# Side work in a planned transformer layer: new prices and gates for the planner, fewer VectorE operations, the first two output blocks in halves

## The chip, the cores and the metric

One core of one Trainium2 chip. The metric is the device time of one execution in microseconds (us); the time of a kernel is the median of its runs. Engine names are those of the profile: PE is TensorE's matmuls and PEld its weight loads, DVE is VectorE, ACT is ScalarE, POOL is GpSimd, SP is SyncE.

## The reference

One inference step of one decoder layer for a prompt of 256 tokens and 8 sample tokens (264 columns in all), in fp32, with a model width of 2048:

```
x = x + W_out[ RGLRU-group(xn) || mLSTM-group(xn) ],  xn = RMSNorm(x), one projection xn @ w_in
x = x + CrossAttn(RMSNorm(x), memory K/V)             (4 heads, 256 memory tokens)
x = x + SwiGLU(RMSNorm(x))
y = RMSNorm_final(x)
```

What the change touches lies in the first line. The RG-LRU group (8 blocks of 128 channels) takes a causal convolution of width 4 over the tokens, two sigmoid gates r and i from block-diagonal matrices, and a linear recurrence:

```
log_a = -8 * r * softplus(-lam);  a = exp(log_a)
mult  = sqrt(max(1 - exp(2 * log_a), 0));  bx = mult * (i * xr)
h_t   = a_t * h_(t-1) + bx_t                 # over the 256 prompt tokens, one step for a sample token
y_rg  = rmsnorm(h * gelu(z_gate), g_rg_out)
```

The mLSTM group (4 heads, keys of 128, values of 256) has an input gate and a log-sigmoid forget gate per token and head, a stabilised chunkwise form for the prompt, and for each sample token one update of a 128 x 256 state:

```
C = sc * C + k v^T;  n = sc * n + k;  h = (q C) / max(|q n|, exp(-m))
y_ml = rmsnorm(h, g_ml_out) * sigmoid(z_o)
```

## The kernel before

All matmuls of the big projections are made in three passes of fp32r: a weight is split into a high part (ScalarE, a copy) and a low part (VectorE, raw minus high), the activations likewise, and `mm3` adds high x high, high x low and low x high. Activations lie transposed, with channels on partitions and the 264 tokens on columns.

The work is a list `steps` of weight blocks. A step is one output block of 128 channels: 16 chunks of 128 x 128, so 48 matmuls of 264 columns. Steps 0 to 3 take the first four recurrence blocks by chunks of the input, steps 4 to 7 the other four, step 8 the mLSTM gates (32 matmuls), 9 to 16 queries and keys, 17 to 24 values, 25 to 32 the RG output gates (`evac_rgg`), 33 to 40 the mLSTM output gates, 41 to 56 the output projection W_out, 57 to 72 the queries of the cross attention. Then follow memory keys and values, the attention's output, and the SwiGLU.

SP loads the blocks ahead (`load_piece`, a ring of five raw half blocks), and `split_half` splits the block of the next step into two of four `w` tiles, at high priority. A finished PSUM bank (four of tag `mm`, four of tag `ax`) is read by the step's evacuation, which is held in `pend` and emitted at the next step.

Everything else is **side work**: Python generators that emit a few instructions at a time between two steps. `rg_gen` makes the recurrence, `ml_gates` the gate sums, `ml_prompt`, `ml_values` and `ml_heads` the prompt's heads, `ml_sample` the 32 sample blocks (8 tokens x 4 heads), `ml_norm` the mLSTM group's norm, `rg_out` the RG group's, `mem_gen` the memory's norm. A generator yields a number after a piece, and `STEP` where it wants to wait for the next step. `Engine` adds a price in us for each instruction to a clock per engine (`price_dve`, `price_act`, `price_pe`); before each step the clocks of DVE and ACT are raised to that of PE, and `pump` lets the generators go on, in the order of their priorities, while both clocks are below PE's clock plus 0.5. Where a step names a `need`, `finish` empties that generator first.

This is the order of emission. The framework's scheduler then orders the instructions on ACT, DVE, PE and POOL by priority along a timeline that it simulates, and sets the semaphores; only SP's order is written by hand. On the chip each engine works its list off in order, so an instruction that waits holds what stands behind it.

Small tiles come from rings: `tmp` from six tiles of tag `t`, `ctile` from eight tiles of 16 columns, and `dw` and `ds` (two each) serve the cross attention of the sample tokens, which starts in the steps after 57.

Places that the change touches: the planner (`price_dve` line 63, `price_act` line 71, `Gen.run` line 275, `pump` line 291); `log1p`; `evac_rgx` and `rg_conv` (lines 491 and 510), which scale a recurrence block out of PSUM and convolve it; `rg_gen` (526); `rg_out` (588), which uses `rstd_wide`: one fp32 matmul with a matrix of ones, and Newton steps over 264 columns, where `rstd_from` sums per token into three columns, does its steps there and spreads the result by matmuls; `evac_if` and `ml_gates`, with rows of 4 heads x 264 tokens; the mask in `ml_prompt`; the temporaries of `ml_sample`; `proj` (930), where the spread of the first norm's factor is put between two chunks of steps 5 and 6; `evac_first`; the steps of W_out; and the main loop (1378).

Of the kernel before, what the change touches and what calls it, by code (L numbers as in the profile page):

```python
# [10 lines left out]
F32 = mybir.dt.float32  # L11
# [6 lines left out]
P = 128  # L18
# [45 lines left out]
def price_dve(name, n, a, k):  # L64
    fast = name in ("tensor_scalar", "tensor_copy", "tensor_single_scalar", "memset")
    if name == "tensor_reduce":
        n = int(np.prod(a[1].shape[1:]))
    return 0.07 + n * (0.00052 if fast else 0.0066 if name == "reciprocal" else 0.00104)


def price_act(name, n, a, k):
    return 0.12 + n * 0.00083

# [7 lines left out]
def layer_kernel(ctx: ExitStack, tc, xT, memT, vec, wrg, w_in, w_out, w_q, w_k, w_v, w_o,  # L81
# [189 lines left out]
    class Gen:  # L271
        def __init__(self, g, prio=0):
            self.g, self.done, self.prio = g, False, prio

        def run(self, go):
            while not self.done and go():
# [5 lines left out]
                if y is STEP:  # L282
                    break

    def side(g, prio=0):
# [5 lines left out]
    def pump(until):  # L291
        go = lambda: dve.clock < until and act.clock < until
        for x in list(gens):
            if x.prio < 0:
                with tc.high_priority():
                    x.run(lambda: True)
# [173 lines left out]
    def log1p(out, e):  # L470

        w = e.shape[-1]
        pp = e.shape[0]
        s = tmp(w)[:pp]
        q = tmp(w)[:pp]
        dve.tensor_scalar(q, e, 2.0, None, op0=OP.add)
        dve.reciprocal(q, q)
        dve.tensor_mul(s, e, q)
        s2 = tmp(w)[:pp]
# [11 lines left out]
    def evac_rgx(n):  # L491
        def f(ps):
            if n == 0:
                rg["xr"] = Arr(RGB)
            z = B([P, 2, 292])
            zi = z[:, 0, :]
            dve.memset(zi[:, 0:3], 0.0)
            smp = zi[:, 259:291].rearrange("p (b j) -> p b j", j=4)
            hist = V("cst", n * 24, 24).rearrange("p (b j) -> p b j", j=3)
            act.activation(smp[:, :, 0:3], hist, AF.Copy)  # L500
            p2, m = unturn(ps[:, :N]), N // 2
            dve.tensor_mul(zi[:, 3: 3 + m], p2[:, 0, :], rstd[:, :m])
            dve.tensor_mul(zi[:, 3 + m: 259], p2[:, 1, : T - m], rstd[:, m:T])
            dve.tensor_mul(smp[:, :, 3:4], p2[:, 1, T - m:].rearrange("p (b j) -> p b j", j=1),
                           rstd[:, T:N].rearrange("p (b j) -> p b j", j=1))
            rg["z", n] = z
            rg["zn"] = n + 1
        return f

    def rg_conv(n):  # L510
        z = rg.pop(("z", n))
        zi, t = z[:, 0, :], z[:, 1, :]
        smp = zi[:, 259:291].rearrange("p (b j) -> p b j", j=4)
# [4 lines left out]
        dve.scalar_tensor_tensor(t[:, :288], zi[:, 1:289], w[1], t[:, :288], op0=OP.mult, op1=OP.add)  # L518
        dve.scalar_tensor_tensor(t[:, :288], zi[:, 2:290], w[2], t[:, :288], op0=OP.mult, op1=OP.add)
        xr = rg["xr"](n)  # L520
        dve.scalar_tensor_tensor(xr[:, :T], zi[:, 3:259], w[3], t[:, :T], op0=OP.mult, op1=OP.add)
        ts = t[:, 259:291].rearrange("p (b j) -> p b j", j=4)
        dve.scalar_tensor_tensor(xr[:, T:N].rearrange("p (b j) -> p b j", j=1), smp[:, :, 3:4], w[3],
                                 ts[:, :, 0:1], op0=OP.mult, op1=OP.add)

    def rg_gen():
# [5 lines left out]
        for n in range(RGB):  # L532
            while rg["zn"] <= n:
                yield STEP
            rg_conv(n)
            yield STEP
            for t, j, b in ((r, 0, "ba"), (ig, 1, "bx")):
                ps = bank("ax")
                pe.matmul(ps[:, :N], wr[j][:, n, :], rg["xr"](n), start=True, stop=True)
                last = act.activation(t(n), ps[:, :N], AF.Sigmoid, bias=V(b, n))  # L540
            yield 0.1
# [4 lines left out]
        for n in range(RGB):  # L546
            with tc.issue_after(last.ins):
                act.activation(e2(n), r(n), AF.Exp, scale=c[:, 8 + n: 9 + n])
                le = act.activation(r(n), r(n), AF.Exp, scale=c[:, n: n + 1])
            dve.tensor_scalar(e2(n), e2(n), 1.0, -1.0, op0=OP.min, op1=OP.add)  # L550
            dve.tensor_mul(ig(n), ig(n), xr(n))
            yield 0.8
        for n in range(RGB):
            with tc.issue_after(le.ins):
                act.activation(e2(n), e2(n), AF.Sqrt, scale=-1.0)
            dve.tensor_mul(ig(n), ig(n), e2(n))
# [65 lines left out]
    def evac_if(ps):  # L622
        R = Arr(7)
        ml["R"] = R
        for q in range(2):
            pool_e.memset(R.tile(q), 0.0)
        li, u, a, b = (R(j)[0:4] for j in range(4))
        act.activation(halves(a), unturn(ps[64:68, :N]), AF.Copy)
        act.activation(halves(b), unturn(ps[96:100, :N]), AF.Copy)
        dve.tensor_add(halves(li), unturn(ps[0:4, :N]), halves(a))  # L630
        dve.tensor_add(halves(u), unturn(ps[32:36, :N]), halves(b))
        dve.tensor_mul(li, li, rstd[0:4, :])
        dve.tensor_mul(u, u, rstd[0:4, :])
        dve.tensor_scalar(li, li, V("bi")[0:4], None, op0=OP.add)
        dve.tensor_scalar(u, u, V("bf")[0:4], None, op0=OP.add)
        ml["gates"] = side(ml_gates(), 1)

    mrow = const.tile([4, 1 + NS], F32, name="mrow")
    gcol = const.tile([P, 2, H], F32, name="gcol")
# [3 lines left out]
    def ml_gates():  # L643
        R = ml["R"]
        li, u, e, lf, b, g, M = (R(j)[0:4] for j in range(7))
        yield STEP
        dve.scalar_tensor_tensor(e, u, -1.0, u, op0=OP.mult, op1=OP.min)
        act.activation(e, e, AF.Exp)
        yield 0.4
        log1p(lf, e)  # L650
        yield 6.0
        dve.tensor_scalar(u, u, 0.0, None, op0=OP.min)
        dve.tensor_sub(lf, u, lf)

# [28 lines left out]
        act.activation(gcol, ps[:, 64:72].rearrange("p (j h) -> p j h", h=H), AF.Copy)  # L683
        act.activation(emc, ps[:, 72:84], AF.Exp, scale=-1.0)
        yield 0.1
# [27 lines left out]
    def ml_prompt():  # L713
# [13 lines left out]
        for h in range(H):  # L727
# [13 lines left out]
            act.activation(E, E, AF.Exp)  # L741
            dve.tensor_mul(E[:, 0:128], E[:, 0:128], mask)
            dve.tensor_mul(E[:, 256:384], E[:, 256:384], mask)
            dve.tensor_mul(Pm, sps[:, 0:384], E)
# [57 lines left out]
    def ml_sample():  # L802
# [127 lines left out]
    def proj(src, rhs, evac, cols=2048, n=N, need=()):  # L930

        def f(i):
# [3 lines left out]
            for c in range(nch):  # L936
                if (i, c) in ((5, 9), (6, 3)):
                    with tc.high_priority():
                        st["rstd_x"].run(lambda: True)
                mm3(ps[:, :n], w(c), rhs(c), c == 0, c == nch - 1)  # L940
# [15 lines left out]
    def evac_first(_):  # L956
        for n in range(4):
            evac_rgx(n)(first[n])
# [93 lines left out]

    for m in range(KC):
        proj(w_out[m], ry, residual(m, "g_xa", "xa", norm_wide),
             need=("rgout", "ng") if m == 0 else ())

# [312 lines left out]
    with tc.high_priority(), in_order():  # L1369
# [4 lines left out]
        split_half(0, 1)  # L1374

    pend = []
    kept = ExitStack()
    for i, (src, cols, pef, evf, need) in enumerate(steps):
        if i > 1:
            load_piece(i + LD - 1)  # L1380
        if i == 7:
            st["rg"] = side(rg_gen(), 0)
        if "ng" in need:
            with tc.high_priority(300):
# [156 lines left out]
```

## Time and profile before

| | us |
|---|---|
| median of 3 runs (lowest to highest) | 1469.44 (1466.56 to 1472.32) |
| the profiled execution | 1467.96 |
| its span, first to last instruction | 1466.2 |
| TensorE busy in it | 1442.1 |
| VectorE busy | 1063.2 |
| ScalarE busy | 790.1 |
| GpSimd busy | 129.5 |
| mean granted clock of TensorE | 0.995 |

The profile is of one execution. A row of a timeline or of a group names engine, operation, the tile written and the tiles read (`w<-raw` is a weight split, `mm<-B,w` a big matmul, `t<-mm,rstd` the evacuation of an RG gate), its shape, a count, and the idle time of the engine ahead of it with what ended that idle time. Times in a timeline are us from the span's start. Almost all instructions are recorded by one helper, so all have the line L60, and tiles tell them apart.

### The profile page before, as it was taken

What the parts mean: (1) busy time and instruction counts of PE and PEld (TensorE: products, weight loads), DVE (VectorE), ACT (ScalarE), POOL (GpSimd) and SP (SyncE); (2) the same over time, 40 slices, a digit from 0 to 9 for tenths busy, and PEclk for the clock granted to TensorE, in tenths of its full rate; (3) what the DMA queues carried; (4) which work ended last, traced back from release to release, by engine and by line L of the source; (5) the groups of instructions that cost most, each with busy time, mean ns of one, the idle gap of its engine ahead of it and who ended that gap; (6) DMA issues with size and microseconds to landing.
All of it is one profiled execution on the core that took longest, in us unless ns stands there. A gap on an engine that the chain in (4) does not pass through costs nothing.

```text
span 1466.2 us, 30098 instructions
## 1 busy us (share of the span) xinstructions
PE 1442.1 (98%) x12049; PEld 1417.3 (97%) x12049; DVE 1063.2 (73%) x2046; ACT 790.1 (54%) x1252; POOL 129.5 (9%) x195
## 2 busy tenths in 40 slices
PE   9998999999999999999999999999999999999997
PEld 8998898999999999999999999999999999999997
DVE  7986788998799999986675656555565655556564
ACT  7566685666466666665544444344444434444463
POOL 0000220000124344320000000000000000000000
PEclk9999999999999999999999999999999999999999
DMA  9654896447699978855555555555555555555563
GB/s 290 212 186 158 271 318 237 169 173 245 247 351 344 342 287 336 343 206 185 195 196 189 199 195 195 201 190 199 192 197 199 190 202 189 199 195 194 174 191 114
DMA packets 99757, 326.02 MB, mean 222 GB/s; under 512 B 10944, under 2 KB 19824, under 8 KB 99616
## 3 DMA queue, kind: packets, MB, share of 16 engines
q1 hardware_dynamic: 83616, 269.84, 52.7%
q0 software_dynamic: 15136, 53.16, 10.0%
q8 instruction: 94, 1.54, 0.4%
q10 hardware_dynamic: 864, 1.09, 0.2%
q14 instruction: 47, 0.39, 0.1%
HBM read 312.78 MB, written 11.28 MB: 221 GB/s over the span
## 4 chain that ended last, share of the span: by engine, by line
PE 92%; DVE 3%; ACT 2%; DMA 2%; issue 1%; SPq 0%; DVEq 0%; ACTq 0%
PE mm L60 87%; PE ax L60 4%; DVE B L60 2%; DVE w L60 1%; DMA raw<-w_in 1%; ACT w L60 1%; ACT B L60 1%; DMA o_sc<-B 0%; DMA B<-scr 0%; DVE t L60 0%; ACT L60 0%; ACT t L60 0%; SPq L199 0%; SPq L1354 0%; DVE c L60 0%
## 5 line engine op out<-in xcount | busy, mean ns | idle before, releaser
L60 PE MATMUL mm<-B,w 128*128 128x264 f32 (+1 forms) x10960 | 1285.9, 279 | 7.1 <-DVE t L60 3.6
L60 PEld LDWEIGHTS mm<-B,w 128*128 128x128 f32 x10960 | 1264.6, 190 | 16.2 <-issue 4.6
L60 DVE TENSOR_TENSOR w<-raw,w 128x1024 fp32r<-128x1024 f32 (+1 forms) x522 | 623.1, 1195 | 298.9 <-ACT w L60 298.2
L60 ACT ACTIVATE w<-raw 128x1024 fp32r<-128x1024 f32 (+1 forms) x522 | 536.2, 1029 | 550.9 <-PE mm L60 381.9
L60 PE MATMUL mm<-w,B 128*128 128x512 f32 x384 | 86.5, 380 | 0.0
L60 PEld LDWEIGHTS mm<-w,B 128*128 128x128 f32 x384 | 70.7, 189 | 9.4
L1433 POOL TENSOR_TENSOR B<-B,rstd 128x264 f32<-128x264 f32 x4 | 2.8, 736 | 802.9 <-ACT rstd L60 802.9
L60 DVE TENSOR_TENSOR t<-mm,rstd 128x264 f32<-128x264 f32 x96 | 41.4, 432 | 28.7 <-PE mm L60 28.7
L60 DVE SCALAR_TENSOR_TENSOR B<-B,dw 128x256 f32<-128x256 f32 x128 | 53.0, 466 | 2.8 <-ACT dw L60 2.6
L60 DVE TENSOR_TENSOR xres<-xres,mm 128x264 f32<-128x264 f32 (+1 forms) x81 | 34.2, 423 | 27.0 <-PE mm L60 27.0
L60 DVE SCALAR_TENSOR_TENSOR dw<-B,qsm,dw 128x256 f32<-128x256 f32 x96 | 49.0, 516 | 0.8
L60 PE MATMUL ax<-B,B 128*128 128x256 f32 (+3 forms) x288 | 46.3, 302 | 1.2 <-DVE B L60 1.2
L1104 POOL TENSOR_TENSOR ds<-dw,ds 128x256 fp32r<-128x256 f32 x32 | 37.5, 1172 | 105.2 <-ACT ds L60 105.1
L60 PEld LDWEIGHTS ax<-B,B 128*128 128x128 f32 x288 | 39.9, 191 | 3.3 <-DVE B L60 1.4
L60 ACT ACTIVATE B<-xres,vecs 128x264 fp32r<-128x264 f32 (+1 forms) x64 | 32.2, 503 | 6.3 <-DVE xres L60 4.6
L60 ACT ACTIVATE t<-xres 128x264 f32<-128x264 f32 (+1 forms) x53 | 21.1, 408 | 15.9 <-DVE xres L60 15.9
L1093 POOL DMA_DIRECT2D B<-kcT x32 | 17.4, 543 | 122.0 <-DVE B L60 109.1
L60 DVE SCALAR_TENSOR_TENSOR B<-xres,vecs,B 128x264 fp32r<-128x264 f32 x48 | 23.3, 486 | 4.1 <-ACT B L60 4.1
L60 ACT ACTIVATE t<-B,B 128x128 f32<-128x128 f32 x64 | 21.4, 390 | 7.4 <-DMA B<-scr 7.3
L60 ACT ACTIVATE dw<-B,qsm 128x256 f32<-128x256 f32 x32 | 16.2, 507 | 16.8 <-issue 7.8
L60 ACT ACTIVATE B<-t 128x264 fp32r<-128x264 f32 (+1 forms) x60 | 24.1, 408 | 1.5 <-DVE t L60 1.5
L60 ACT ACT_TABLE_LOAD x18 | 23.1, 1283 | 2.6 <-PEq L1513 1.7
(168 smaller groups left out, 689.2 us busy)
## 6 DMA issues: line engine op xcount, KB each, us to landing
raw<-w_gu SPq DMA_DIRECT2D x176, 512.0 KB, 3.7
raw<-w_d SPq DMA_DIRECT2D x80, 512.0 KB, 3.7
raw<-w_in SPq DMA_DIRECT2D x74, 512.0 KB, 4.6
raw<-w_out SPq DMA_DIRECT2D x32, 512.0 KB, 4.1
B<-kcT POOLq DMA_DIRECT2D x32, 512.0 KB, 8.8
raw<-w_q SPq DMA_DIRECT2D x32, 512.0 KB, 4.4
B<-vcT POOLq DMA_DIRECT2D x32, 512.0 KB, 9.8
raw<-w_k SPq DMA_DIRECT2D x32, 512.0 KB, 5.3
```

The source lines that it names most:

```text
L60: return f(*a, **k)
L1093: pool_e.dma_start(kc, kcT[h, b])
L1104: pool_e.tensor_sub(ws[:, 1], acc, ws[:, 0].bitcast(F32))
L1433: e.tensor_mul(st["y"](c), st["y"](c), r)
```

## The change

It does the following.

- **Planner.** The prices get rates for reciprocal and scan, a larger fixed part for `scalar_tensor_tensor` and for accumulating operations, for a per-partition scale on ScalarE, and 1.28 for a change of ScalarE's function table. They hold up to step 57; after it the old ones come back. A generator is now stopped only by the clock of an engine that its last piece used, and after a `STEP` its first piece always goes.
- **Recurrence.** An evacuation reads the bank in one product instead of three, the first product of the convolution goes to ScalarE, `1 - exp(2 log_a)` becomes a Relu on ScalarE, the memsets go to POOL. Two blocks are convolved in one step, and their four sigmoids follow together.
- **mLSTM gates.** Both gates are scaled in one tile of 36 partitions; the log-sigmoid is made after a turn by matmuls, on 12 columns, and turned back. The exponential of `emc` moves to the first head of `ml_prompt`.
- **Norm of the RG group** by `rstd_from`; **mask** by one operation a head; **sample blocks** take their temporaries from `dw` and `ds`.
- **First norm.** Its factor is spread at chunk 8 of step 6 instead of chunk 3, and the bank of tag `mm` is read first.
- **W_out.** Blocks 0 and 1 first take their RG chunks (0 to 7); only then is the mLSTM norm finished, and the other chunks of both follow.

The diff, cut:

```diff
 def price_dve(name, n, a, k):
...
+    rate = {"reciprocal": 0.0066, "tensor_tensor_scan": 0.00208}.get(name, 0.00052 if fast else 0.00104)
+    fixed = 0.12 if name == "scalar_tensor_tensor" else 0.07
+    return fixed + n * rate + (0.08 if "accum_out" in k else 0.0)
...
 def price_act(name, n, a, k):
-    return 0.12 + n * 0.00083
+    func, load = a[2] if len(a) > 2 else k.get("func"), 0.0
+    if func in (AF.Exp, AF.Sqrt, AF.Sigmoid, AF.Gelu_apprx_tanh, AF.Silu) and func != TABLE["at"]:
+        TABLE["at"], load = func, 1.28
+    by_column = not isinstance(k.get("scale", 1.0), (int, float))
...
+    return load + (0.2 if by_column else 0.12) + n * 0.00083 + (0.2 if "accum_out" in k else 0.0)
...
-        go = lambda: dve.clock < until and act.clock < until
+        go = lambda used: not (used[0] and dve.clock >= until or used[1] and act.clock >= until)
...
     def evac_rgx(n):
...
-            dve.memset(zi[:, 0:3], 0.0)
+            pool_e.memset(zi[:, 0:3], 0.0)
...
-            dve.tensor_mul(zi[:, 3: 3 + m], p2[:, 0, :], rstd[:, :m])
-            dve.tensor_mul(zi[:, 3 + m: 259], p2[:, 1, : T - m], rstd[:, m:T])
-            dve.tensor_mul(smp[:, :, 3:4], ...)
+            dve.tensor_mul(halves(zi[:, 3: 3 + N]), unturn(ps[:, :N]), halves(rstd))
+            act.activation(smp[:, :, 3:4], zi[:, 3 + T: 3 + N].rearrange("p (b j) -> p b j", j=1), AF.Copy)
...
     def rg_conv(n):
...
-        dve.tensor_scalar(t[:, :288], zi[:, 0:288], w[0], V("cb", n), op0=OP.mult, op1=OP.add)
+        act.activation(t[:, :296], zi[:, 0:296], AF.Identity, scale=w[0], bias=V("cb", n))
...
     def rg_gen():
...
             rg_conv(n)
+            yield 1.5
+            if n % 2 == 0:
+                continue
             yield STEP
-            for t, j, b in ((r, 0, "ba"), (ig, 1, "bx")):
+            for q in (n - 1, n):
+                for t, j, b in ((r, 0, "ba"), (ig, 1, "bx")):
...
-            dve.tensor_scalar(e2(n), e2(n), 1.0, -1.0, op0=OP.min, op1=OP.add)
+                act.activation(e2(n), e2(n), AF.Relu, scale=-1.0, bias=ones[:, 0:1])
...
     def rg_out():
-        yield from rstd_wide(acc_rg, rr, RGB * P)
+        yield from rstd_from(acc_rg, rr, RGB * P)
...
     def ml_gates():
+        for j, w0 in enumerate(WIN):
+            pe.matmul(ps[:, 4 * j: 4 * j + 4], R(0)[:, w0: w0 + P], ident[:, 32:36], start=True, stop=True)
...
+        for j, (lo, hi) in enumerate(((0, P), (P, T), (T, N))):
+            pe.matmul(ps[0:4, lo:hi], lu[:, 4 * j: 4 * j + 4], ident[:, P - (hi - lo):], start=True, stop=True)
...
     def ml_sample():
-                    t2 = tmp(256).rearrange("p (v d) -> p v d", d=P)
+                    t2 = sb.tile([P, 264], F32, tag="dw", bufs=2, name=nm("dw"))[:, 0: T]
...
-                    j = tmp(P)
+                    j = sb.tile([P, 2, T], F32R, tag="ds", bufs=2, name=nm("ds"))[:, 0, 0: P].bitcast(F32)
...
-                if (i, c) in ((5, 9), (6, 3)):
+                if (i, c) in ((5, 9), (6, 8)):
...
+    def pe_out(m):
+        def f(i):
+            ps, w = bank(), W(i)
+            kept_out[m] = (ps, w)
+            for c in range(RGB):
+                mm3(ps[:, :N], w(c), ry(c), c == 0, False)
+            if m == 1:
+                finish(lambda: st["ng"].done)
+                for c in range(RGB, KC):
+                    for q in range(2):
+                        mm3(kept_out[q][0][:, :N], kept_out[q][1](c), ry(c), False, c == KC - 1)
+            return ps
...
+        if i == 57:
+            PACE["full"] = False
```

More of the change, by code (lines that the diff above doesn't have):

```diff
@@ L272, in __init__ @@
         def __init__(self, g, prio=0):
-            self.g, self.done, self.prio = g, False, prio
+            self.g, self.done, self.prio, self.used = g, False, prio, (False, False)
         def run(self, go):
-            while not self.done and go():
+            while not self.done and go(self.used):
+                was = dve.clock, act.clock
                 try:
@@ L282, in run @@
                 if y is STEP:
+                    self.used = False, False
                     break
+                self.used = dve.clock > was[0], act.clock > was[1]
     def side(g, prio=0):
@@ L626, in evac_if @@
             pool_e.memset(R.tile(q), 0.0)
[L627 to L636, printed above, removed]
+        x, a = R(0)[0:36], R(1)[0:36]
+        act.activation(gbias[0:4], V("bi")[0:4], AF.Copy)
+        act.activation(gbias[32:36], V("bf")[0:4], AF.Copy)
+        act.activation(halves(a), unturn(ps[64:100, :N]), AF.Copy)
+        dve.tensor_add(halves(x), unturn(ps[0:36, :N]), halves(a))
+        dve.tensor_mul(x, x, rstd[0:36, :])
+        dve.tensor_scalar(x, x, gbias[0:36], None, op0=OP.add)
+        ml["gates"] = side(ml_gates(), 0)
+    gbias = const.tile([P, 1], F32, name="gbias")
+    pool_e.memset(gbias, 0.0)
     mrow = const.tile([4, 1 + NS], F32, name="mrow")
@@ L644, in ml_gates @@
         R = ml["R"]
[L645 removed]
+        li, e, lf, b, g, M = (R(j)[0:4] for j in (0, 2, 3, 4, 5, 6))
         yield STEP
[L647 to L648 removed]
+        ps = bank("ax")
+        for j, w0 in enumerate(WIN):
+            pe.matmul(ps[:, 4 * j: 4 * j + 4], R(0)[:, w0: w0 + P], ident[:, 32:36], start=True, stop=True)
+        u, eu, lu = ctile(12), ctile(12), ctile(12)
+        act.activation(u, ps[:, 0:12], AF.Copy)
+        dve.scalar_tensor_tensor(eu, u, -1.0, u, op0=OP.mult, op1=OP.min)
+        act.activation(eu, eu, AF.Exp)
         yield 0.4
[L650 to L651 removed]
+        log1p(lu, eu)
         dve.tensor_scalar(u, u, 0.0, None, op0=OP.min)
[L653 removed]
+        dve.tensor_sub(lu, u, lu)
+        yield 2.0
+        yield STEP
+        ps = bank("ax")
+        for j, (lo, hi) in enumerate(((0, P), (P, T), (T, N))):
+            pe.matmul(ps[0:4, lo:hi], lu[:, 4 * j: 4 * j + 4], ident[:, P - (hi - lo):], start=True, stop=True)
+        act.activation(lf, ps[0:4, :N], AF.Copy)
         one = ones[0:4, 0:1].to_broadcast([4, T])
@@ L956, in evac_first @@
     def evac_first(_):
-        for n in range(4):
+        for n in (3, 0, 1, 2):
             evac_rgx(n)(first[n])
@@ L1051, in ry, with evac_out, g @@
         return st["yrg"](c) if c < 8 else st["yml"](c - 8)
-    for m in range(KC):
-        proj(w_out[m], ry, residual(m, "g_xa", "xa", norm_wide),
-             need=("rgout", "ng") if m == 0 else ())
+    kept_out = {}
+    def pe_out(m):
[10 more added lines that the diff above has]
+            return ps
+        return f
+    def evac_out(m):
+        f = residual(m, "g_xa", "xa", norm_wide)
+        def g(ps):
+            if m == 1:
+                residual(0, "g_xa", "xa", norm_wide)(kept_out[0][0])
+            if m > 0:
+                f(ps)
+        return g
+    for m in range(2):
+        steps.append((w_out[m], 2048, pe_out(m), evac_out(m), ("rgout", "pend") if m == 0 else ()))
+    for m in range(2, KC):
+        proj(w_out[m], ry, residual(m, "g_xa", "xa", norm_wide))
     qn = {"n": 0}
@@ L1374, in layer_kernel @@
         split_half(0, 1)
+    PACE["full"], TABLE["at"] = True, None
     pend = []
```

55 lines of the change are left out of this document (30 added, 25 removed).

## The prediction

> **What bounds the kernel now.** I read the busy times of the whole span first, then TensorE's waits, then stretches around them, then the instructions there. The windows view, its columns the busy time of each engine with the instructions in brackets, then the granted clock, the DMA share and GB/s:
>
> ```profile
> core 0: us, PE busy (x) PEld busy (x) DVE busy (x) ACT busy (x) POOL busy (x), PEclk, DMA share, GB/s
> 0.00:1466.20 1466.20, 1442.08 (x12049) 1417.25 (x12049) 1063.21 (x2046) 790.05 (x1252) 129.47 (x195) 1.00 0.63 222
> 121.60:135.40 13.80, 9.66 (x58) 8.79 (x58) 11.66 (x25) 9.54 (x18) 0.00 (x0) 0.75 0.25 87
> 231.10:240.40 9.30, 9.25 (x57) 7.59 (x58) 7.63 (x22) 6.37 (x18) 2.66 (x5) 0.84 0.67 232
> ```
>
> TensorE is busy for 1442.1 of 1466.2 us, so no other engine's saved work can count by itself. Only TensorE's waits, and what follows from them, can be won. The view of waits for TensorE (total, times, longest):
>
> ```profile
> PE ax L60 <- DVE B L60: 4.0, 3, 1.7
> PE mm L60 <- DVE t L60: 3.6, 1, 3.6
> PE mm L60 <- ACT w L60: 2.0, 1, 2.0
> PE ax L60 <- ACT w L60: 1.9, 3, 1.1
> PE ax L60 <- DVE c L60: 1.6, 1, 1.6
> PE mm L60 <- DVE w L60: 1.5, 2, 1.1
> ```
>
> TensorE's timeline shows where they lie (start, us, instructions, idle time before with its releaser):
>
> ```profile
> 44.39 0.81 PE L60 MATMUL ax<-ident,c 128*128 128x128 f32 x6 [1.56 <-DVE c L60]
> ...
> 128.75 0.90 PE L60 MATMUL ax<-ident,B 128*128 128x128 f32 x3 [1.07 <-DVE B L60]
> 129.31 0.79 PE L60 MATMUL mm<-B,w 128*128 128x264 f32 x2
> 131.19 15.19 PE L60 MATMUL mm<-B,w 128*128 128x264 f32 x116 [1.10 <-DVE w L60]
> ...
> 205.73 21.85 PE L60 MATMUL mm<-B,w 128*128 128x264 f32 x192
> 231.15 5.47 PE L60 MATMUL mm<-B,w 128*128 128x264 f32 x34 [3.57 <-DVE t L60]
> ...
> 263.78 2.07 PE L60 MATMUL ax<-ident,c 128*128 128x128 f32 x18
> 265.71 38.05 PE L60 MATMUL mm<-B,w 128*128 128x264 f32 x336
> ```
>
> The run of 192 gives the undisturbed price: 21.85 / 192 = 0.1138 us a matmul, 48 x 0.1138 = 5.46 us a step. Four losses stand out, all inside the first projection (steps 0 to 40).
>
> **A**, in step 6: 1.56 us, TensorE waits for the last small VectorE operation of the RMS factor.
>
> **B**, in step 19: the waits of 2.0 (ACT w), 1.07 and 1.10, together 4.2 us. Then the clock: it was granted at 0.75 in that window, and 116 matmuls took 15.19 where 116 x 0.1138 = 13.20 would do, 2.0 us more. B is 6.2.
>
> **C**, in steps 25 and 26: what is left of the first row, 4.0 - 1.07 = 2.9 us.
>
> **D**, ahead of step 33: 3.57 us; then 34 matmuls in 5.47 instead of 3.87 at a clock of 0.84, 1.6 us. D is 5.2.
>
> Sum: 1.6 + 6.2 + 2.9 + 5.2 = 15.9 us. This is about all that the change can reach; from 265.71 on, 336 matmuls run without a wait, over the start of the output projection (three steps later, near 282).
>
> Here the trace and the Trainium skill differ. "TensorE: Matmul & The Clock Gate", section "HAM oscillation", speaks of no idle gaps over about 3.4 us. In B the clock fell although its longest single gap is 2.0, so the sum of gaps seems to count. By the rule B would hold no clock loss, and the forecast below would be 2.0 us smaller.
>
> **Why B happens.** ScalarE's timeline:
>
> ```profile
> 119.58 1.04 ACT L60 ACTIVATE w<-raw 128x1024 fp32r<-128x1024 f32 x1
> 120.53 1.72 ACT L60 ACTIVATE B<-B,rgc 128x264 f32<-128x264 f32 x4
> 122.27 1.28 ACT L60 ACT_TABLE_LOAD   x1
> 123.56 2.30 ACT L60 ACTIVATE B<-B 128x264 f32<-128x264 f32 x7
> 125.77 1.04 ACT L60 ACTIVATE w<-raw 128x1024 fp32r<-128x1024 f32 x1
> ```
>
> Two weight splits (w<-raw) lie 6.2 us apart, more than a whole step, with recurrence work and a table load between them. The planner prices these exponentials at 0.34 us and the load at nothing; measured are 1.72 / 4 = 0.43 and 1.28. It believes that there is room and emits too much into one step.
>
> **Why D happens.** VectorE's timeline, then the operations on tile bcs (count, duration, first and last start):
>
> ```profile
> 230.58 0.43 DVE L60 TENSOR_TENSOR t<-mm,rstd 128x264 f32<-128x264 f32 x1
> ```
>
> ```profile
> L60 DVE SCALAR_TENSOR_TENSOR B<-B,bcs,t x32: 475/479/486, 159.6 to 233.1; 128x256 f32<-128x256 f32 x32
> ```
>
> The first row is the evacuation of step 29, whose matmuls were the first 48 of the 192 and ended near 211.2. It came 19 us later, and without it no PSUM bank was free for step 33 (four banks). It waited for nothing that the row names. I take it to be the ring of six "t" tiles: the gate's z, the mLSTM sample blocks' t2 and their product j all come out of it, and in that stretch each block takes two.
>
> **The change, part by part.**
>
> *Spread from chunk 3 to chunk 8 of step 6.* Fifteen matmuls, 1.7 us, go ahead of the waiting one. The wait of 1.56 is covered: -1.6. The evacuations behind it start no later, since the chain on VectorE ends when it did.
>
> *t2 and j moved to the tiles dw and ds.* Nothing else uses these before the queries' projection. The ring holds only gate work then, and D goes whole: -5.2. The price is two buffers in place of six: ScalarE's t2 of one block waits for VectorE's use of two blocks before. VectorE is the slower of the two, so I take 0; if not, it falls under the second rival.
>
> *Prices, gates, pairs.* VectorE's groups (mean ns):
>
> ```profile
> L60 DVE TENSOR_TENSOR w<-raw,w 128x1024 fp32r<-128x1024 f32 x488 | 599.8, 1231 | 294.8 <-ACT w L60 294.1
> ...
> L60 DVE SCALAR_TENSOR_TENSOR t<-B,B 128x128 f32<-128x128 f32 x64 | 18.4, 288 | 1.5
> ...
> L60 DVE DVE_READ_ACCUMULATOR t<-B,B 128x1 f32 x64 | 5.2, 81 | 0.0
> ...
> L60 DVE TENSOR_SCALAR B<-B,vecs 128x288 f32<-128x288 f32 x8 | 3.1, 422 | 0.0
> ...
> L60 DVE TENSOR_SCALAR B<-B 128x264 f32<-128x264 f32 x8 | 2.4, 298 | 2.1 <-ACT B L60 1.4
> ```
>
> A sample block was priced 0.336 + 2 x 0.203 = 0.742 and is now 0.386 + 2 x 0.333 = 1.052; measured is 0.479 + 2 x (0.288 + 0.081) = 1.22. A step leaves VectorE, by the planner, 5.47 - 2.27 for two splits - 0.35 for an evacuation = 2.85 us. That was 3.8 blocks a step, 4.7 us of real work, beside two splits of 1.23 and an evacuation of 0.43: 7.6 us asked of 5.46. With the new price it is 2.7 blocks, 3.3 us, 6.2 in all: still over, by much less, and the rows are durations, which overlap by some 0.1 us. So C shrinks but I doubt that it goes: I take its longest wait, -1.7, and leave 1.2. In B the exponentials become 0.42 each and the load 1.28, so the burst spreads over three steps; both ScalarE's wait and VectorE's wait for w should go, and with them the clock loss, while the 1.07 behind DVE B is a chain of its own: -5.1.
>
> *Fewer VectorE operations.* The convolution's first product (8 x 0.422 = 3.4 us) and the subtraction (8 x 0.298 = 2.4) move to ScalarE; log1p runs over 12 columns instead of 264. VectorE's saved time counts nothing by itself: TensorE's work hides it, outside B and C. ScalarE takes 16 operations of about 0.43, 6.9 us over a dozen steps, and some small copies. Also hidden if spread; if they land ahead of a split, second rival. Eight 3-column memsets go to POOL, idle in that window: 0.
>
> *More matmuls.* The gates' two turns (6 fp32 matmuls) and the RG group's norm by columns (6) give 24 short TensorE instructions; six such took 0.81 at 44.39, and spaced at 0.1138 24 make 2.7 us. The one wide sum they replace is not set off. +2.7, with 0 (they fall into waits) and 3.2 as ends.
>
> *Two output blocks in halves.* There is no wait at 282 to cover: 0 now. It costs nothing either, unless all four w tiles being held delays step 43; its first half is free after 24 matmuls and has 72 (8.2 us) to be split.
>
> Sum: -1.6 - 5.2 - 1.7 - 5.1 + 2.7 = -10.9 us. The profiled execution took 1467.96, so 1457.1; the median of the runs stands 1.5 above it, which makes **1458.5**. If all four losses go and the matmuls are free, 1469.4 - 15.9 = 1453.5.
>
> **Rivals.** *ScalarE becomes late instead.* The page "ScalarE: Activation LUTs" of the Trainium skill, section "Rules for kernel authors", wants relu, mul and add on VectorE; that speaks against this move. In rows: ahead of a split like that at 125.77 stand eight more operations of 0.43, 3.4 us. Then B and C stay, A and D go: -1.6 - 5.2 + 2.7 = -4.1, 1465.3; with B deeper by 3.4, 1468.7. For it: ScalarE was the releaser of B. Against it: the new prices count these operations. About 1467, no change.
>
> *The sample blocks starve (slower).* Blocks now run from 159.6 to 233.1, 73.5 us; the norm's spreads follow at 263.78, 31 us later, and the output projection needs them by 282 + 5.5 for the half steps = 287.5, less some 8 us for the products after the spreads: 16 us of slack. The dearer price alone stretches 73.5 by 1.052 / 0.742 to 104, 31 us more. Then TensorE waits 15 us in step 42 and loses 2.0 by the clock as in B: -10.9 + 17 = +6.1, 1475.5, and more if dw and ds slow it too. It decides at 16 us of delay. For it: prices only rise. Against it: blocks were held up by the ring and by bursts, not by their price alone, since 32 in 73.5 us are 2.4 a step, below the 2.7 that the new price allows.
>
> **How the numbers follow.** The forecast, with all-gone as its best end: 0.68, faster. ScalarE late: 0.18, same. Starving: 0.10, of which 0.06 over the bound and 0.04 within. Not named: 0.04, slower. Half a per cent, 7.3 us, is about what a measurement can tell here, so faster is 0.68, same 0.22, slower 0.10. The range runs from 1452 (all-gone, with half the 3 us by which the lowest run lies under the median) to 1470, which takes in ScalarE late with 1.3 for the same spread.
>
> **What would show it.** Right: no wait <-DVE t; the eight gate evacuations each within a step of their matmuls; no ACT stretch of 6 us between splits near the Exp; the clock at 1.00 from 60 to 280; the last sample block before 250. Wrong: the wait at 44.39 moved instead of gone; TensorE waiting for ACT w or DVE B for over 4 us in sum; a wait in the second half of step 42.

## The result, and the profile after

| | before | after |
|---|---|---|
| median of 5 runs, us (lowest to highest) | 1469.44 (1466.56 to 1472.32) | 1456.42 (1455.83 to 1456.79) |
| ratio, 95% interval | | 0.9915 (0.9900 to 0.9929) |
| the profiled execution, us | 1467.96 | 1455.83 |
| its span, us | 1466.2 | 1454.1 |
| mean granted clock of TensorE | 0.995 | 0.998 |

The changed kernel is 13.0 us faster by the medians, 12.1 us by the profiled executions. The forecast was 1458.5, in a range of 1452 to 1470. The runs also lie closer together: 1.0 us apart instead of 5.8. One of the eleven runs of a kernel below, that with the ring undone, took 3921.74 us and is left out of its ratio.

The windows view of after, for the whole span and for the window of B:

```profile
0.00:1460.00 1460.00, 1439.19 (x12071) 1415.52 (x12071) 1045.10 (x1999) 794.90 (x1279) 128.31 (x204) 1.00 0.63 223
121.60:135.40 13.80, 11.89 (x100) 11.35 (x99) 13.38 (x27) 8.72 (x18) 3.42 (x7) 1.00 0.66 183
```

In the second row 100 matmul instructions stand where before had 58, and the clock is 1.00 where it was 0.75. Nowhere between the start and 1449.7 us is a clock under 1.00 granted. Before had two stretches at 0.5 there: 6.8 us from 128.2 and 3.4 us from 230.6.

The view of TensorE's waits (total, times, longest):

```profile
PE mm L60 <- DVE w L60: 2.1, 2, 1.9
PE ax L60 <- ACT w L60: 2.1, 3, 1.5
PE mm L60 <- DVE ones L60: 1.1, 1, 1.1
PE ax L60 <- DVE B L60: 0.8, 1, 0.8
```

With two more of 0.3 this sums to 6.7 us; before it was 16.0. The wait for `t` (D) and that for `c` of 1.56 (A) are gone, the waits for `B` fell from 4.0 to 0.8. TensorE's timeline shows the four places:

```profile
44.08 0.73 PE L60 MATMUL ax<-ident,c 128*128 128x128 f32 x6
...
71.50 0.73 PE L60 MATMUL ax<-ident,B 128*128 128x4 f32 x6
...
82.48 0.64 PE L60 MATMUL ax<-ident,c 128*4 128x128 f32 x6
...
124.25 0.38 PE L60 MATMUL ax<-ident,B 128*128 128x128 f32 x2
126.52 3.19 PE L60 MATMUL mm<-B,w 128*128 128x264 f32 x26 [1.89 <-DVE w L60]
...
154.50 1.14 PE L60 MATMUL ax<-B,B 128*128 128x258 f32 x4 [0.81 <-DVE B L60]
...
188.18 43.45 PE L60 MATMUL mm<-B,w 128*128 128x264 f32 x384
231.46 0.72 PE L60 MATMUL ax<-ones,acc_rg 128*128 128x1 f32 x6
...
239.49 0.73 PE L60 MATMUL ax<-ident,c 128*128 128x128 f32 x6
```

The spread at 44.08 has no idle time ahead of it (A). At 126.52 one wait of 1.89 is left of B, at 154.50 one of 0.81 of C. At 188.18 stand eight whole steps without a wait, 43.45 / 384 = 0.113 us a matmul, over the place of D. The rows of six at 71.50, 82.48, 231.46 and 239.49 are the new short matmuls (E).

So the account of the span: waits 16.0 - 6.7 = 9.3 us; 10.2 us at half clock lose half, 5.1, less some 1.1 that were waits themselves (0.5 us of the wait of 1.07, all of that of 1.10 and 0.5 us of that of 3.57 lie inside the stretches, and half of these 2.2 us would count twice); and 1.5 back for matmul time, as the comparison with the kernel of four parts below gives it. 9.3 + 4.0 - 1.5 = 11.8 of the 12.1.

### The profile page after: what moved, and what is told of

Its sections match the earlier page's. It is cut to its first block, busy times and chain, and to the rows that moved or that the text cites. A ratio compares the mean times of both kernels' runs of the same rounds, so it can differ in the third digit from the quotient of the medians.

```text
span 1454.1 us, 30126 instructions
## 1 busy us (share of the span) xinstructions
PE 1439.2 (99%) x12071; PEld 1415.5 (97%) x12071; DVE 1045.1 (72%) x1999; ACT 794.9 (55%) x1279; POOL 128.3 (9%) x204
## 3 DMA queue, kind: packets, MB, share of 16 engines
q0 software_dynamic: 15136, 53.16, 10.2%
## 4 chain that ended last, share of the span: by engine, by line
PE 94%; ACT 2%; DMA 1%; DVE 1%; issue 1%; SPq 0%; POOL 0%; DVEq 0%; POOLq 0%
PE mm L60 90%; PE ax L60 5%; DMA raw<-w_in 1%; ACT B L60 1%; DVE B L60 1%; DMA B<-scr 0%; ACT w L60 0%; DVE w L60 0%; ACT L60 0%; SPq L213 0%; ACT dw L60 0%; DVE ds L60 0%; SPq L1412 0%; DMA scr<-lt 0%; ACT t L60 0%
## 5 line engine op out<-in xcount | busy, mean ns | idle before, releaser
L60 PEld LDWEIGHTS mm<-B,w 128*128 128x128 f32 x10960 | 1260.6, 189 | 10.7 <-DVE w L60 2.4
L60 ACT ACTIVATE dw<-B,B 128x128 f32<-128x128 f32 x64 | 20.9, 390 | 7.1 <-DMA B<-scr 6.3
L60 ACT ACTIVATE dw<-ax,dw 128x256 f32<-128x256 f32 x32 | 15.0, 470 | 17.7 <-DVE dw L60 14.0
```

Source lines behind the costliest of these rows:

```text
L60: return f(*a, **k)
```

## The experiments

The question was which parts make the gain. The theory of the forecast adds losses that are independent of each other: the ring cures D, chunk 8 cures A, the prices cure B and C. Its rivals: the parts need each other; the exponentials merely move; the sample blocks starve. First four parts were done alone on the kernel before, then parts were undone one by one in the kernel after, then a set of four was put on before. The gate alone was not run, nor the pairs or the halves alone. In all, ratios are to the kernel before on the same chip, with 95% intervals; where runs on different chips are set side by side, it is by these ratios. A ratio on record is not the quotient of the two medians; the two differ by up to 0.0012, 1.8 us.

**The ring alone** (on before; the same for `j`, on `ds`):

```diff
-                    t2 = tmp(256).rearrange("p (v d) -> p v d", d=P)
+                    t2 = sb.tile([P, 264], F32, tag="dw", bufs=2, name=nm("dw"))[:, 0: T]
+                    t2 = t2.rearrange("p (v d) -> p v d", d=P)
```

> The kernel before, with only the two temporaries of the sample blocks moved from the six-tile ring t to the tiles dw and ds. My theory (the ring holds back the gate evacuations): the wait of 3.57 us behind DVE t goes, the eight gate evacuations come within a step of their matmuls, no half clock after it; about 5.2 us less, 1464 against 1469. Rival (VectorE is simply over-asked by underpriced blocks): the evacuations stay 9 to 19 us late, 0 us.

Measured: 1465.30 us, ratio 0.9969 (0.9958 to 0.9981), which is 4.6 us. The wait for `t` is gone, and the sample blocks run faster than before, to 218.1 instead of 233.1:

```profile
L60 DVE SCALAR_TENSOR_TENSOR B<-B,bcs,dw x32: 473/478/485, 158.1 to 218.1; 128x256 f32<-128x256 f32 x32
```

So D was the ring, and two buffers do not slow the blocks. C, with 2.56 us in sum hardly smaller than before (2.88), now has one wait of 2.02. TensorE's timeline, then the window just behind that wait:

```profile
179.31 4.09 PE L60 MATMUL ax<-B,B 128*128 128x256 f32 x12 [2.02 <-DVE B L60]
```

```profile
179.40:182.60 3.20, 3.20 (x10) 2.75 (x11) 3.20 (x12) 2.21 (x4) 0.24 (x1) 0.50 0.74 252
```

A half-clock stretch of 3.4 us, which D had before, stands here now, and takes back a part of the gain.

**Chunk 8 alone** (on before):

```diff
-                if (i, c) in ((5, 9), (6, 3)):
+                if (i, c) in ((5, 9), (6, 8)):
```

> The kernel before, with only the spread of the first norm's factor put at chunk 8 of step 6. My theory: the wait of 1.56 us goes and nothing follows it, 1.6 us less. Rival (the first evacuations come later by as much and TensorE waits for a bank in steps 7 to 9): the wait moves, 0 us.

Measured: 1468.84 us, ratio 0.9990 (0.9978 to 1.0002). The wait at 44 is gone from its trace, but the time shows it only as a hint: in the profiled execution, the longest of its runs, the half-clock stretch of B lasts 10.2 us instead of 6.8, one more of 3.4 stands at 176.7, and that of D lasts 6.8. A cured wait of 1.56 is within what these stretches vary by.

**The prices alone** (on before, up to step 57 as in the change: `price_dve`, `price_act` and the switch `PACE`; gate, operations and tiles as before):

> The kernel before, with only the new price functions (up to step 57); the gate of the planner, the operations and the rings stay. My theory (waits B and C come from work emitted too densely because it is underpriced): B loses 5.1 of its 6.2 us and C 1.7 of 2.9, so about 6.8 less; D stays, since the ring stays. Rival (the number of VectorE operations sets B and C): 0 us.

Measured: 1469.23 us, ratio 0.9997 (0.9988 to 1.0007), 0.4 us where 6.8 were expected. Most of B and all of D are gone: the longest wait at B's place is 1.07, and no wait for `t` is left although the ring is the old one. What they brought was paid back. The operations on `bcs`, TensorE's timeline, and the window behind the wait:

```profile
L60 DVE SCALAR_TENSOR_TENSOR B<-B,bcs,t x32: 471/478/485, 158.4 to 274.2; 128x256 f32<-128x256 f32 x32
```

```profile
272.12 2.74 PE L60 MATMUL mm<-B,w 128*128 128x264 f32 x22 [1.22 <-DVE w L60]
...
288.17 5.29 PE L60 MATMUL ax<-ident,c 128*128 128x128 f32 x24 [6.03 <-DVE c L60]
```

```profile
285.70:295.70 10.00, 7.54 (x33) 7.36 (x34) 8.20 (x28) 2.23 (x5) 0.00 (x0) 0.50 0.11 37
```

The sample blocks take 115.8 us instead of 73.5. The mLSTM norm behind them comes late, TensorE waits 6.03 us for its factor ahead of the output projection, and 10.2 us at half clock follow. This is the rival of starving.

**The operations alone** (on before: the convolution's and the recurrence's products on ScalarE, log1p on 12 columns, the RG norm by columns, the mask in one operation; planner, chunk, ring, one block a step and whole output blocks as before):

> The kernel before, with only the changed operations: one product in the evacuation, first product of the convolution and the Relu on ScalarE, log1p on 12 columns after a turn, the RG norm by columns, one mask operation; planner, rings, spread, one block a step and whole output blocks as before. My theory: VectorE's time is not what bounds, TensorE gets 2.7 us more work, so 0 to 3 us more. Rival (fewer VectorE operations cure B and C): 5 us less.

Measured: 1475.60 us, ratio 1.0038 (1.0025 to 1.0052), 5.6 us slower. That is more than the 0 to 3 us expected, and the rival, a gain of 5, is refuted. One reading is that a planner that prices too low fills the room with more work. This run does not show it separately: it also carries the short matmuls, the work moved to ScalarE, another order of the first evacuations and a higher priority for the gates' generator. TensorE's timeline:

```profile
183.50 2.09 PE L60 MATMUL ax<-B,B 128*128 128x258 f32 x4 [4.85 <-DVE B L60]
...
236.32 3.88 PE L60 MATMUL mm<-B,w 128*128 128x264 f32 x18 [3.57 <-DVE t L60]
```

The four alone sum to -4.6 - 1.5 - 0.4 + 5.6 = -0.9 us (-4.8 by the medians); the whole brings 12.5 by its ratio. The gate is missing from this sum, so it does not show by itself that the parts do not add; the same part alone and undone does, below.

**The gate undone** (after, with the old rule: a generator goes on only while both clocks are below the limit):

```diff
-        go = lambda used: not (used[0] and dve.clock >= until or used[1] and act.clock >= until)
+        go = lambda used: dve.clock < until and act.clock < until
```

> The changed kernel with the planner's old gate (a generator stops when either clock is over, and its first piece after a STEP may be refused). New theory, from the prices alone: dearer prices starve the sample blocks (they ended at 274 there, TensorE waited 6 us for the norm), and the new gate is what starts them 20 us earlier. Then they start after 150 and end after 245 here, TensorE waits for DVE c in step 42, 1464 to 1468. Rival (pairs and fewer operations start them earlier): they start near 137 as in the changed kernel, 1456 to 1458.

Measured: 1465.53 us, ratio 0.9978 (0.9964 to 0.9993): all but some 3 us of the gain is lost, 9 us. The sample blocks start 24.7 us later than in after and take 86.0 us instead of 70.8 (first row this kernel, second row after):

```profile
L60 DVE SCALAR_TENSOR_TENSOR B<-B,bcs,dw x32: 471/478/485, 161.3 to 247.3; 128x256 f32<-128x256 f32 x32
L60 DVE SCALAR_TENSOR_TENSOR B<-B,bcs,dw x32: 468/476/486, 136.6 to 207.4; 128x256 f32<-128x256 f32 x32
```

Three kinds of waits, for `w` (4.1 us in 7), `B` (3.6) and `c` (2.1), come back. The one for `c` stands in step 36, where the RG norm's factor is spread, not in step 42, where it was expected for the mLSTM norm. The runs reach from 1463.65 to 1472.83, and the profiled one, 1471.45, is one of the long ones. The edit undoes both halves of the gate, the condition for each engine and the first piece after a `STEP`; no run parts them.

**The prices undone** (after, with the old ones throughout):

```diff
-    PACE["full"], TABLE["at"] = True, None
+    PACE["full"], TABLE["at"] = False, None
```

> The changed kernel with the old prices throughout. The prediction's theory (prices thin out B and C): B and C come back, 6.8 us more, 1463. Rival (the prices alone did nothing, and the new gate and the pairs did the work): 1456 to 1458.

Measured: 1465.87 us, ratio 0.9964 (0.9952 to 0.9976): by the ratios 7 us are lost. The sample blocks keep their place (137.1 to 204.1), but the heads are crowded: the view of TensorE's waits

```profile
PE ax L60 <- DVE B L60: 5.1, 3, 2.1
PE ax L60 <- ACT B L60: 2.6, 2, 2.0
```

and two half-clock stretches of 3.4 us, from 158.9 and from 172.6. That is C and more. B does not come back, though: between 110.88 and 139.93 TensorE has no wait. So the 7 us are near the 6.8 expected, but half of the account behind them fails.

**The ring undone** (after, with `t2` and `j` from `tmp` again):

> The changed kernel with the sample blocks' temporaries back on the ring t. The prediction's theory: D comes back, 5.2 us more, 1461.6. Rival, from the prices alone, where the gate evacuations were prompt on the old ring: blocks that are spaced by the new prices leave the ring free, 0 to 1 us more.

Measured: 1469.72 us, ratio 0.9991 (0.9980 to 1.0001). Next to nothing of the gain is left, against both expectations (5.2 us lost, or 0 to 1). The ring is worth 4.6 us alone, and by the two ratios 11 here (0.9915 and 0.9991). The operations on `bcs`, then a row of TensorE's timeline:

```profile
L60 DVE SCALAR_TENSOR_TENSOR B<-B,bcs,t x32: 476/479/485, 136.2 to 250.5; 128x256 f32<-128x256 f32 x32
```

```profile
168.45 2.09 PE L60 MATMUL ax<-B,B 128*128 128x258 f32 x4 [2.56 <-DVE B L60]
```

The blocks start early, as the gate lets them, and then take 114.3 us. The old ring serves them and the gates' evacuations, which come at 190 to 251 instead of 180 to 221. D's own wait does not come back at its size: TensorE waits 0.87 us for `t`. Between the two profiled executions lie 13.0 us: 6.4 more of waits, the largest 2.56 (above) and 2.07 in step 54, and 10.2 us at half clock, which lose 5.1. Of these, 3.4 us at half clock stand behind a wait that after has as well (last section), so some 1.7 us are not the ring's.

**The halves undone** (after, with output blocks 0 and 1 whole):

> The changed kernel with output blocks 0 and 1 whole, the norm finished before step 41. The prediction's theory: no wait there to cover, 0 us. Rival: what is left of the norm's chain after step 40 is exposed, 3 to 6 us more.

Measured: 1457.32 us, ratio 0.9910 (0.9896 to 0.9924). The halves bring nothing that can be measured.

**Four parts on before**: prices, gate, ring and chunk 8, by the edits above, and nothing else of the change.

> The kernel before with four parts of the change alone: the prices, the gate per engine, the ring (t2 and j on dw and ds) and chunk 8. Left as before: all operations (convolution and subtraction on VectorE, log1p on four rows, the wide norm sum), one recurrence block a step, output blocks whole. Additive theory (each part brings what it brought alone: -4.6, -0.4, -0.6, and the gate 0): about 1464 for a before of 1470. Theory of interaction (prices, gate and ring work only together, and the operations only thin the work): the sample blocks start before 150 and end before 225, no half clock between 60 and 280, time within 3 us of the changed kernel, 1455 to 1460. If it is below 1455, the 24 extra matmuls of the operations cost more than their thinner work brings.

Measured: 1456.94 us, ratio 0.9901 (0.9888 to 0.9915). That is the whole gain, without one moved operation, pair or half. The mechanism that was expected did not show in one point: the sample blocks start at 157.1, not before 150. So the gate by itself does not start them early; with the changed operations it does, even without the pairs (138.9, below). They need no early start here, since they take only 53.9 us:

```profile
L60 DVE SCALAR_TENSOR_TENSOR B<-B,bcs,dw x32: 472/480/486, 157.1 to 211.0; 128x256 f32<-128x256 f32 x32
```

ScalarE's timeline of this kernel shows what became of B:

```profile
104.25 1.28 ACT L60 ACT_TABLE_LOAD   x1
105.55 4.98 ACT L60 ACTIVATE B<-B,rgc 128x264 f32<-128x264 f32 x12
110.43 1.04 ACT L60 ACTIVATE w<-raw 128x1024 fp32r<-128x1024 f32 x1
```

The burst of twelve exponentials is still there, ahead of one split. It comes earlier by 9 us (at 105.55, where before had it at 114.70), and TensorE waits 0.38 and 0.77 us behind it instead of 4.2.

Do the parts add? The additive theory reached about 1464 with the gate at 0, which no run has measured. But whatever the gate brings alone, a part that adds is worth the same alone and undone, and the ring is worth 4.6 and 11 us, the prices 0.4 and 7, differences beyond the intervals. Without the prices, the gate or the ring, 5.3, 3.2 or 1.3 of the 12.5 us are left. So they need each other; how much the gate brings alone stays open.

**The subtraction back on VectorE** (after; the root's scale is -1 again):

```diff
-                act.activation(e2(n), e2(n), AF.Relu, scale=-1.0, bias=ones[:, 0:1])
+            dve.tensor_scalar(e2(n), e2(n), 1.0, -1.0, op0=OP.min, op1=OP.add)
```

> The changed kernel with the eight subtractions of the recurrence back on VectorE (0.30 each there) in place of Relu on ScalarE (0.4 each). Theory that ScalarE is what is late in the remaining wait of 1.89 us in step 19: that wait shrinks or goes, time 1454 to 1456.5. Rival, that VectorE is the scarcer engine around the recurrence, as the move assumes: waits <-DVE w or <-DVE B of 2 to 4 us and perhaps a half-clock stretch, 1458 to 1461. If neither, within 1 us of the changed kernel's 1456.4.

Measured: 1456.94 us, ratio 0.9904 (0.9889 to 0.9918). Neither theory fits whole. The wait of 1.89 in step 19 is gone, as the first had it, but one of 2.07 for ScalarE stands a step earlier, in step 18, and the time is the same. TensorE's timeline, and the window behind the wait:

```profile
120.91 0.49 PE L60 MATMUL mm<-B,w 128*128 128x264 f32 x2 [2.07 <-ACT w L60]
```

```profile
122.20:125.40 3.20, 3.20 (x15) 3.20 (x16) 3.20 (x5) 2.29 (x3) 0.00 (x0) 0.50 0.56 188
```

The clock is halved here, and the runs spread over 4.5 us (1454.64 to 1459.10) where after spreads over 1.0.

**The RG norm by a wide sum again** (after):

```diff
-        yield from rstd_from(acc_rg, rr, RGB * P)
+        yield from rstd_wide(acc_rg, rr, RGB * P)
```

> The changed kernel with the recurrence's output norm again by one wide sum on TensorE and some dozen VectorE operations of 264 columns, in place of 12 short matmuls and small columns. It prices half of the +2.7 us that the forecast put on the short matmuls: by that term 1455 to 1455.5 (12 fewer of 0.11 each, one wide fp32 sum more). Rival: the VectorE operations, about 3.6 us, land in the stretch where the gate evacuations share their ring, and cost a wait: 1457.5 to 1460.

Measured: 1456.55 us, ratio 0.9898 (0.9884 to 0.9911), between the two expectations. Beside the other kernels of the same chip (1455.08 to 1456.94) twelve short matmuls cannot be told from none.

**One recurrence block a step** (after):

```diff
-            yield 1.5
-            if n % 2 == 0:
-                continue
             yield STEP
-            for q in (n - 1, n):
...
```

> The changed kernel with one recurrence block a step, as before, and not two. The forecast put nothing on the pairs by themselves. If so, within 1 us of 1456.4, with the exponentials one to three steps later. Rival: the pairs halve the steps of the recurrence's gates, so without them the exponentials fall some 20 us later, the sample blocks begin after 150 and the time rises by 3 to 8 us with a wait in steps 25 to 42.

Measured: 1455.08 us, ratio 0.9889 (0.9876 to 0.9903). The exponentials and the sample blocks (138.9 to 206.5) hardly move, so the pairs gain nothing. If anything they cost: the wait of B is shorter here and that at 154 is gone.

```profile
126.60 5.56 PE L60 MATMUL mm<-B,w 128*128 128x264 f32 x47 [1.47 <-DVE w L60]
```

This is the lowest median of all kernels, and its highest run, 1455.62, lies below the lowest of after. But the two ran on different chips, and by the ratios their intervals just overlap, so that it beats after is not shown.

## Why the prediction was right

**The bound and the four places.** Right. TensorE's busy time hardly moved (1442.1 to 1439.2), and the gain is the waits and the clock, as listed. Of the forecast's signs, the wait for `t`, the clock from 60 to 280 and the last sample block (207.4, before 250) came as it said. VectorE's saved work brought nothing that shows: the operations alone, with the matmuls and the ScalarE work that come with them, made the kernel slower, and the four parts have the whole gain without them.

**A**, -1.6: the wait is gone, and the steps start 2.07 us earlier by step 7 (47.45 for 49.52). Alone, in the time, it could not be told from nothing.

**B**, -5.1 of 6.2: -1.97, -1.07, -1.10 and the clock's 2.0 went, and 1.89, 0.34 and 0.21 came, so about -3.7. This is the term that was sized too large, and its mechanism was only half right. The forecast had the exponentials spread over three steps. ScalarE's timeline of after shows them still close together:

```profile
103.23 1.06 ACT L60 ACTIVATE w<-raw 128x1024 fp32r<-128x1024 f32 x1 [1.64 <-PE mm L60]
...
108.51 3.76 ACT L60 ACTIVATE B<-B,rgc 128x264 f32<-128x264 f32 x9
...
115.01 1.04 ACT L60 ACTIVATE w<-raw 128x1024 fp32r<-128x1024 f32 x1
...
118.80 1.04 ACT L60 ACTIVATE w<-raw 128x1024 fp32r<-128x1024 f32 x1
...
122.83 1.04 ACT L60 ACTIVATE w<-raw 128x1024 fp32r<-128x1024 f32 x1
```

Exponentials and Relus fill 108.51 to 115.01, 6.5 us, and with the table loads and sigmoids ahead of them no split is made from 104.29 to 115.01, 10.7 us. That is against the forecast's own sign ("no ACT stretch of 6 us"). Nor was the stretch that the forecast showed for before, 5.2 us between two splits, the longest there. The one ahead of it, 111.22 to 119.58, is 8.4 us long:

```profile
110.16 1.06 ACT L60 ACTIVATE w<-raw 128x1024 fp32r<-128x1024 f32 x1 [1.59 <-PE mm L60]
...
114.70 4.97 ACT L60 ACTIVATE B<-B,rgc 128x264 f32<-128x264 f32 x12
```

The longer stretch in after did not hurt: splits then follow each 4 us, and TensorE waits 0.34 and 0.21. So B did not shrink by spreading the burst, and the low prices are not shown to be its cause: its waits are 1.78 us with the prices alone, 2.05 with the operations alone, neither with a half-clock stretch, and none with the prices undone. What cures B in after is open. The 1.89 that are left wait for VectorE: the high part of that split was done on ScalarE by 123.87, and VectorE's timeline of after has two scans of the recurrence ahead of the low part.

```profile
124.08 1.27 DVE L60 TENSOR_TENSOR_SCAN B<-B,B 128x256 f32<-128x256 f32 x2
125.27 1.20 DVE L60 TENSOR_TENSOR w<-raw,w 128x1024 fp32r<-128x1024 f32 x1
```

**C**, -1.7 of 2.9: 0.81 is left, so -2.1. Right, and the prices bear on it as forecast: alone they bring it to 1.4 (0.22 and 1.18), and with the old ones the waits for `B` grew to 7.7 us in all. They are not enough, since 2.56 stand there with the ring undone.

**D**, -5.2: gone whole, and the ring was the cause; the part alone shows it. What the forecast did not see is that prices alone remove this wait too, by thinning the blocks, and that the ring's larger worth lies in the combination: without it the blocks take 114.3 us instead of 70.8.

**E**, +2.7: the four groups took 0.73 + 0.64 + 0.72 + 0.73 = 2.82 us, and the wide sum that went takes 0.61 in the kernel of four parts, so 2.2 net; by TensorE's busy time after has 1.5 more than the kernel of four parts (1439.19 and 1437.73). The size was about right, and no difference in time could be told.

**Halves**, 0: right.

**The sum**: -1.6 - 3.7 - 2.1 - 5.2 + 2.2 = -10.4 by the same terms, where -10.9 was forecast and -12.1 measured. By the account of the span above, the rest is some tenths each of smaller waits, half clock and matmul time. Between two single executions no more can be said: the runs of before lie 5.8 us apart. That the sum came so near is in part luck. It adds parts that do not add: the 6.8 us that it put on the prices, gates and pairs (B 5.1, C 1.7) were 0.4 with the prices alone, and came out only with the ring and the gate beside them. The size of B, 1.4 too large, was made up for by C and E (0.4 and 0.5) and by tenths that the sum does not name.

**ScalarE late**: it did not happen. Eight Relus on it or not made no difference in time. The Trainium skill's rule for relu, mul and add on VectorE ("ScalarE: Activation LUTs", section "Rules for kernel authors") would not have bought anything here, for relu at least, the one that was tried.

**Starving**: the gap in the working. Its mechanism and its place were right, as the prices alone show: 115.8 us, more than the 104 forecast, and a late factor ahead of the output projection, at 8 us of waits where 15 were put on it. The argument against it ("held up by the ring and by bursts") was not sufficient: with ring and prices but the old gate the blocks still take 86.0 us. What held the rival off are ring and gate together: with the new gate but the old ring the blocks take 114.3 us, and with both and the prices 53.9 to 71.3 in six kernels. The forecast named the ring here, but on the gate by itself it put no number. The gate replaced "both clocks below the limit" by "the clock of the engine that was used", so that a generator whose last piece left ScalarE alone is not stopped by ScalarE's clock; that this is how it helps the blocks is read from the code, not shown. The gate's part in this is one that the forecast's argument against the rival did not name.

**What is open**: that the ring is worth so much more in the combination is shown by the times and the spans of the blocks; how each wait follows from it is not. The gate was not run alone. Whether the four parts could be three was tried only from the other side: prices, gate and ring cannot be left out of after, and chunk 8 was not left out.

## What to carry to other kernels

In these kernels, side work that was priced too low crowded the heads (C), and dearer prices alone starved what follows; a new price needs a look at the gate and at the buffers that set the pace under it, and the three are worth measuring together. Undoing each part in the whole tells more than doing each alone: here ring and prices bring 4.6 and 0.4 us one by one, and prices, gate and ring cost 7 to 11 each when undone, of 12.5 in all. Where TensorE is the bound, look for waits of 2 us and the clock behind them before counting another engine's operations.

## What the runs showed of the hardware

Outside the last microseconds the half clock was granted in stretches of 3.4, 6.8 or 10.2 us, and each stood at a wait of TensorE of about 1.8 us or more, or at two or three smaller ones close together: one of 2.02 was enough (the ring alone), and so was one of 2.07 (the subtraction). The Trainium skill ("TensorE: Matmul & The Clock Gate", section "HAM oscillation") speaks of idle gaps over about 3.4 us; these rows contradict it, as B did. Near 2 us it can go either way: a wait of 2.07 at 354.19 with the ring undone and one of 1.98 at 194.87 with the prices undone had no such stretch behind them. In the kernel with the ring undone the wait of after stands once more (first row below is its timeline), and the windows behind it, first of that kernel, then of after, differ:

```profile
126.35 4.86 PE L60 MATMUL mm<-B,w 128*128 128x264 f32 x26 [1.88 <-DVE w L60]
```

```profile
127.30:130.60 3.30, 3.30 (x17) 3.30 (x17) 3.30 (x8) 1.79 (x6) 1.19 (x3) 0.50 0.56 190
```

```profile
126.60:130.00 3.40, 3.40 (x29) 3.35 (x30) 3.40 (x8) 3.32 (x7) 0.56 (x1) 1.00 0.43 164
```

The same 26 matmuls take 4.86 us there and 3.19 in after. Such stretches, which come or stay away from run to run, would explain why the kernels that have one in their trace mostly spread over 4.5 to 9.2 us in their runs, and those that have none over 1.0 to 2.4. Two kernels speak against it, the operations alone (2.6) and the prices undone (2.2), and the kernels differ in their number of runs, from 4 to 12. For the kernel before, the mean clock granted in each run bears it out. Of its 29 runs beside the first four experiments, the 15 at 0.992 took 1470.94 to 1473.19 us, and the 14 at 0.993 to 0.995 took 1467.04 to 1470.04. Why a stretch comes in one run and stays away in another is not shown.
